# Weight sums of a Winograd down projection made ahead during the up projection and kept in HBM, with another order of its products

## The chip, the cores and the metric

The kernel runs on one core of one Trainium2 chip. The metric is the device time of one execution in microseconds (us), as the median of several runs. A profile is one further execution, recorded by the hardware profiler, with its own time.

## The reference

The reference is a two-layer encoder trunk on x of 1024 tokens by 1024 channels in float32. Each layer is a mixer and then a gated feed-forward part; the change touches only the latter:

```
def conv_ffn(h, w_up, conv_w, conv_b, w_down):        # D_FF = 2816
    z = causal_dwconv(h @ w_up, conv_w, conv_b)       # width 3 along the tokens
    a, g = jnp.split(z, 2, axis=-1)
    return (jax.nn.silu(g) * a) @ w_down
x = x + conv_ffn(rms_norm(x, ffn_norm_g[l]), ...)     # l = 0, 1
```

## The kernel before

**Products.** Activations are held transposed: channels on the 128 partitions, tokens along the free dimension, in two halves of 512 tokens (h = 0, 1). Every float32 operand is split in a high part (a cast to fp32r, on ACT) and a low part (source minus high part, on DVE or POOL), and a product is three matmuls: high by high, high by low, low by high (`matmul3`, L328). So each operand costs ACT a cast and DVE or POOL a subtraction.

**Seven products in place of eight.** The two large matrix products of the feed-forward part are done as 2x2 block products in Winograd's form, with seven products, numbered p = 1 to 7, of sums of blocks of both operands. In the up projection (`up`, L508) one `Quad` makes one channel tile j of the value and of the gate (22 quads a layer, NF = 22); a quad is seven products of 12 matmuls. POOL makes the weight sums (L363 to L369) and all low parts of weights (L353), ACT the high parts (L352). DVE evicts: `qe_u` (L402) and `c_u` (L409, the program's c22) add partial sums, then the width-3 convolution is one ACT instruction (L542) and two DVE instructions (L544) for each part and half, three single-column ACT instructions at the border of the halves (L561), and the gate is an ACT sigmoid (L565) and two DVE products for each half (L566, L567). The gated tile z goes to HBM (`hid_d`, L569). Product p=4 of a quad accumulates in the bank `qb` that `c_u` reads, so it waits for `c_u`.

**The down projection** (`down`, L583) reads the gated tiles back. Its contraction runs over NP = 11 pairs of channel tiles, i; one step (p, i) is four output tiles q of three matmuls, 12 matmuls. Order: products 1 and 5 interleaved (5 lags by two steps), then 6 and 3 the same way, then 7, 2, 4. The operands:

- `hidden(i)` (L588) loads both tiles of a pair with both halves at once, 2 x 512 KB, in the first two products; 22 tiles then stay in SBUF. `operand` (L644) makes the sums of blocks on DVE, in place (`hid<-hid`), and the split (`set`, L318 and L319).
- `operand_w` (L611) loads blocks of the weight, 256 KB each (`d<-in_w_down`). For p = 5, 6 and 3 it also makes sums of blocks: one POOL addition for 5; a POOL and a DVE subtraction for 6, and a store of one sum to HBM (L633) that p = 7 loads again; one POOL subtraction for 3. Each product's weights get a cast (L640) and a low part on POOL.

Tiles come from rings: 4 raw weight tiles and 8 split ones (two pools each, taken in turn), 3 tiles `z`, 28 activation tiles. In PSUM the accumulator A uses the tags qa and qb, B uses qe and pp, two banks each.

**What sets the order.** Tile's scheduler orders each engine's instructions at build time, mostly in the order of the program, with earlier places for work that it finds ready; an engine then runs its list strictly in order. Loads and stores sit in one list, SP's (a few of the program's first loads in ACT's). `later(n, fn)` puts work into the program after n further steps (a step is three matmuls in the feed-forward part), `sooner(n)` raises a priority.

Of the kernel before, what the change touches and what calls it, by code (L numbers as in the profile page):

```python
# [17 lines left out]
P = 128  # L18
# [23 lines left out]
NORM_LAG = ((8, 10), (6, 5))  # L42
EPS = 1e-6
# [24 lines left out]
def trunk_kernel(ctx: ExitStack, tc: tile.TileContext, a: dict, out: bass.AP):  # L68
# [11 lines left out]
    now = {"turn": {}}  # L80

    @contextmanager
    def stage(name, psum):

        with (
            tc.tile_pool(name=name, bufs=1, reuse_waits="tile") as mp,
            tc.tile_pool(name=f"ps_{name}", bufs=psum, space=PSUM, reuse_waits="tile") as pp,
        ):
            now.update(mp=mp, pp=pp)
            yield mp  # L90
# [16 lines left out]
    def ps(name):  # L107
        return now["pp"].tile([P, HS], F32, tag="pp", name=name)
# [336 lines left out]
    def run_quads(quads, n_early):  # L445
        for i, q in enumerate(quads[:n_early]):
            q.ready(i == 0)
        for q in quads[:n_early]:
            q.early()
        for q in quads[:n_early]:  # L450
            q.late()
        n = len(quads)
        order = [(n_early, 1), (n_early, 5)]
        for i in range(n_early, n):
            order += [(i, 6), (i, 2), (i + 1, 1), (i, 7), (i, 3), (i + 1, 5), (i, 4)]
        for i, p in order:
            if i < n:
                quads[i].step(p)
# [49 lines left out]
    def up(layer, sets, hid_d):  # L508
# [15 lines left out]
        def evict(j):  # L524
# [10 lines left out]
            def fn(part, h, src):  # L535
# [26 lines left out]
                if len(done) == 4:  # L562
                    for h in range(2):
                        sg = ps(f"sg{layer}_{j}{h}")
                        nc.scalar.activation(sg, z[1][h], AF.Sigmoid)  # L565
                        nc.vector.tensor_tensor(sg, z[1][h], sg, op=ALU.mult)  # L566
                        nc.vector.tensor_tensor(z[0][h], z[0][h], sg, op=ALU.mult)  # L567
                    if j < NF - 2:
                        nc.sync.dma_start(hid_d[j], z[0][2])  # L569
                    else:  # L570
                        stores.append(lambda: nc.sync.dma_start(hid_d[j], z[0][2]))
# [3 lines left out]
        run_quads([Quad(f"u{layer}_{j}", load(j), sets, evict(j)) for j in range(NF)], EARLY)  # L575
        return stores

# [5 lines left out]
    def down(layer, hid_d, nxt, fin, stores):  # L583
        A, B = [[None] * 4 for _ in range(2)]
        hid, two_raw, s2 = {}, {}, {}
        s3_d = [tc.dram_tile([P, HS], F32, name=f"s3_{layer}_{i}") for i in range(NP)]

        def hidden(i):  # L588

            if i not in hid:  # L590
                b = []
                for f in (2 * i, 2 * i + 1):
                    t = actp.tile([P, 2, HS], F32, tag="act", name=f"hid{layer}_{f}")
                    nc.sync.dma_start(t, hid_d[f])
                    b += [t[:, 1], t[:, 0]]
                hid[i] = b
            return hid[i]

        def raw(tag, srcs, name):
            t = ffn_buf(tag, F32, f"d{name}_{layer}")  # L600
            for k, src in enumerate(srcs):
                made = nc.sync.dma_start(t[:, k], src)
            return t, made

        def block(r, c, i):
            return a["w_down"][layer, r, c, i]

        def tt(eng, o, one, two, op=ALU.subtract):
            eng.tensor_tensor(o, one, two, op=op)  # L609

        def operand_w(p, i):  # L611

            if p in (1, 2, 4, 7):

                if i % 2 == 0:
                    ii = range(i, min(i + 2, NP))
                    srcs = [s3_d[k] if p == 7 else block(*{1: (0, 0), 2: (0, 1), 4: (1, 1)}[p], k) for k in ii]
                    two_raw[p], made = raw("raw", srcs, f"{p}_{i}")
                    if stores and i == 2:
                        with tc.issue_after(made.ins):  # L620
                            while stores:
                                stores.pop(0)()
                src = two_raw[p][:, i % 2]
            elif p == 5:
                t, _ = raw("raw", [block(1, 0, i), block(1, 1, i)], f"5_{i}")
                src = t[:, 0]
                tt(nc.gpsimd, src, src, t[:, 1], ALU.add)
            elif p == 6:
                t, _ = raw("raw", [block(0, 0, i), block(1, 0, i)], f"6_{i}")
                z, _ = raw("z", [block(1, 1, i), block(0, 1, i)], f"3_{i}")  # L630
                s3, src = t[:, 0], t[:, 1]
# [3 lines left out]
                s2[i] = z[:, 1], src  # L635
            else:
                src, s2_i = s2.pop(i)
                tt(nc.gpsimd, src, src, s2_i)
            t = ffn_buf("hl", F32R, f"w{p}_{layer}_{i}")
            nc.scalar.copy(t[:, 0], src)  # L640
            tt(nc.gpsimd, t[:, 1], src, t[:, 0].bitcast(F32))
            return t[:, 0], t[:, 1]

        def operand(p, i):  # L644
            b11, b12, b21, b22 = hidden(i)
            if p == 5:
                tt(nc.vector, b11, b12, b11)
            elif p == 6:
                tt(nc.vector, b11, b22, b11)
            elif p == 7:  # L650
                tt(nc.vector, b12, b22, b12)
            src = {1: b11, 5: b11, 6: b11, 3: b22, 7: b12, 2: b21, 4: b21}[p]
            s = {p: []}
            put_set(s, p, src, nc.vector)
            if p == 2:
                tt(nc.vector, b21, b21, b11)
# [7 lines left out]
        def step(p, i):  # L664
            O, first = {1: (A, True), 6: (A, False), 7: (A, False), 5: (B, True), 3: (B, False), 2: (B, True)}[p]
            first = first and i == 0
            W, X = operand_w(p, i), operand(p, i)
            for q in range(4):
                if first:
                    tag = (("qa", "qa", "qb", "qb"), ("qe", "qe", "pp", "pp"))[O is B][q]  # L670
# [17 lines left out]
        def two(p, r, after_p, after_r):  # L688
            for i in range(NP + 2):
# [4 lines left out]
                if i >= 2:  # L694
                    step(r, i - 2)
            after_r()

        def x12():
            takes(A, 0, 0)
# [3 lines left out]
        for i in range(NP):  # L703
            step(7, i)
        takes(A, 1, 0, True)
        for i in range(NP):
            step(2, i)
        takes(B, 0, 1, True)
# [4 lines left out]
        for i in range(NP):  # L713
            ops.append((operand_w(4, i), operand(4, i)))
            if i < tail:
                for q in range(4):
                    product(q, A, *ops[i], False, False)
# [6 lines left out]
    def ffn(layer, sets, nxt, fin):  # L724
        hid_d = [tc.dram_tile([P, 2, HS], F32, name=f"hid{layer}_{j}") for j in range(NF)]
        with (
# [4 lines left out]
            stores = up(layer, sets, hid_d)  # L731
            down(layer, hid_d, nxt, fin, stores)
# [431 lines left out]
```

## Time and profile before

| | |
|---|---|
| median of 3 runs | 1938.11 us (1936.58 to 1938.32) |
| profiled execution | 1944.7 us, of which the span from first to last instruction 1943.0 us |
| granted TensorE clock, mean | 0.979 of full speed |
| busy: PE, DVE, ACT, POOL | 95%, 61%, 48%, 67% of the span |
| DMA | 200.22 MB, mean 103 GB/s |

The two feed-forward parts run from about 289 to 966 us and from about 1259 to 1926 us. In layer 0 the first matmul of the down projection starts at 726.9 us and the last at 965.8 us; in layer 1 at 1689.6 and 1925.5 us. PE's busy time is modelled, because matmuls overlap in its pipeline: a matmul of 512 columns shows as 0.39 us long, and at full clock one starts every 0.2267 us. So lost time is found by counting matmuls in a stretch, not by the busy share.

### The profile page before, as it was taken

The numbers are of one execution on the slowest core, as the hardware profiler recorded it, in microseconds if no ns is written. First come the engines' busy times: TensorE is split into PE (matmuls) and PEld (weight loads), VectorE is DVE, ScalarE is ACT, GpSimd is POOL, SyncE is SP. The second block draws the span as 40 slices with busy tenths as digits, with TensorE's granted clock in tenths as the row PEclk, the third lists the DMA queues.
The fourth block names the chain that finished last, engine by engine and source line by source line (L and its number), as shares of the span: only waits on it lengthen the run. The fifth ranks groups of instructions, "written<-read, shape, count | busy, mean of one in ns | idle before, by whom it ended". The sixth has DMA issues, their size and how long they took to land. (4 is left out here: it accounts for less than half of the span.)

```text
span 1943.0 us, 22672 instructions
## 1 busy us (share of the span) xinstructions
PE 1849.3 (95%) x8088; PEld 1508.5 (78%) x8092; DVE 1190.0 (61%) x1540; ACT 930.7 (48%) x1684; POOL 1302.4 (67%) x946
## 2 busy tenths in 40 slices
PE   8999889999999997999999999999999999798997
PEld 6777667888888876778778888878888888686786
DVE  5899788455554586768620256584555554957784
ACT  6436445555555563345321233365555555532451
POOL 2899567877777775885432446587777777658851
PEclk8999989999999998999999999999999999999998
DMA  4111130222222267543111323202122222865432
GB/s 152 44 54 33 44 98 23 88 96 76 88 82 81 90 233 241 188 145 111 49 54 48 95 86 119 87 30 90 67 96 76 87 85 78 291 216 181 131 98 87
DMA packets 79395, 200.22 MB, mean 103 GB/s; under 512 B 8497, under 2 KB 9521, under 8 KB 79281
## 3 DMA queue, kind: packets, MB, share of 16 engines
q1 hardware_dynamic: 78992, 198.48, 30.5%
q8 instruction: 64, 1.05, 0.2%
q14 instruction: 51, 0.41, 0.1%
q10 hardware_dynamic: 288, 0.28, 0.0%
HBM read 165.70 MB, written 33.03 MB: 102 GB/s over the span
## 5 line engine op out<-in xcount | busy, mean ns | idle before, releaser
L353 POOL TENSOR_TENSOR w_u<-S_u,w_u 128x512 fp32r<-128x512 f32 x160 | 207.4, 1296 | 113.2 <-ACT w_u L352 110.7
L609 POOL TENSOR_TENSOR w<-d,w 128x512 fp32r<-128x512 f32 x154 | 234.3, 1537 | 72.9 <-ACT w L640 72.6
L329 PE MATMUL p<-set,w 128*128 128x512 f32 x616 | 244.2, 396 | 29.7 <-ACT z L561 19.3
L331 PE MATMUL p<-set,w 128*128 128x512 f32 x616 | 243.3, 395 | 6.1 <-POOL w L609 6.1
L330 PE MATMUL p<-set,w 128*128 128x512 f32 x616 | 243.8, 396 | 1.8 <-DVE set L319 1.6
L319 DVE TENSOR_TENSOR set<-hid,set 128x512 fp32r<-128x512 f32 x154 | 162.7, 1077 | 58.3 <-ACT set L318 57.8
L353 POOL TENSOR_TENSOR w_u<-r_u,w_u 128x512 fp32r<-128x512 f32 x120 | 156.1, 1302 | 58.1 <-ACT edge L555 42.4
L329 PE MATMUL qb_u<-set,w_u 128*128 128x512 f32 x480 | 188.4, 393 | 6.4 <-DVE c_u L409 6.3
L331 PE MATMUL qb_u<-set,w_u 128*128 128x512 f32 x480 | 188.2, 392 | 0.0
L330 PE MATMUL qb_u<-set,w_u 128*128 128x512 f32 x480 | 188.0, 392 | 0.0
L640 ACT CAST w<-d 128x512 fp32r<-128x512 f32 x154 | 94.4, 618 | 178.5 <-DVE d L609 105.4
L329 PEld LDWEIGHTS p<-set,w 128*128 128x128 f32 x616 | 117.4, 191 | 59.0 <-ACT z L561 20.2
L544 DVE SCALAR_TENSOR_TENSOR z<-qb_u,cols,z 128x511 f32<-128x511 f32 x88 | 65.8, 748 | 142.0 <-ACT z L542 140.6
L331 PEld LDWEIGHTS p<-set,w 128*128 128x128 f32 x616 | 117.4, 191 | 33.5 <-POOL w L609 9.3
L352 ACT CAST w_u<-S_u 128x512 fp32r<-128x512 f32 x160 | 98.5, 616 | 93.1 <-PE qb_u L331 60.1
L330 PEld LDWEIGHTS p<-set,w 128*128 128x128 f32 x616 | 117.3, 190 | 29.1 <-DVE set L319 5.2
L331 PE MATMUL qa_u<-set,w_u 128*128 128x512 f32 x320 | 124.6, 389 | 0.6 <-POOL w_u L353 0.6
L329 PE MATMUL qa_u<-set,w_u 128*128 128x512 f32 x320 | 124.6, 389 | 0.0
L330 PE MATMUL qa_u<-set,w_u 128*128 128x512 f32 x320 | 124.5, 389 | 0.0
L329 PE MATMUL qe_u<-set,w_u 128*128 128x512 f32 x320 | 124.5, 389 | 0.0
L330 PE MATMUL qe_u<-set,w_u 128*128 128x512 f32 x320 | 124.5, 389 | 0.0
L331 PE MATMUL qe_u<-set,w_u 128*128 128x512 f32 x320 | 124.5, 389 | 0.0
(241 smaller groups left out, 4729.1 us busy)
## 6 DMA issues: line engine op xcount, KB each, us to landing
d<-in_w_down SPq DMA_DIRECT2D x198, 256.0 KB, 3.0
r_u<-in_w_up SPq DMA_DIRECT2D x88, 512.0 KB, 3.3
hid<-z SPq DMA_DIRECT2D x44, 512.0 KB, 2.6
hid<-hid SPq DMA_DIRECT2D x44, 512.0 KB, 5.5
r_wv<-in_od_in SPq DMA_DIRECT2D x16, 512.0 KB, 3.8
r_odo<-in_od_out SPq DMA_DIRECT2D x16, 512.0 KB, 3.3
s<-d SPq DMA_DIRECT2D x22, 256.0 KB, 3.0
d<-s SPq DMA_DIRECT2D x22, 256.0 KB, 3.8
```

Of the source, the lines that this page charges most:

```text
L319: leng.tensor_tensor(t[:, 1], src, t[:, 0].bitcast(F32), op=ALU.subtract)
L329: nc.tensor.matmul(o, H, xH, start=first, stop=False, skip_group_check=True)
L330: nc.tensor.matmul(o, H, xL, start=False, stop=False, skip_group_check=True)
L331: nc.tensor.matmul(o, L, xH, start=False, stop=last, skip_group_check=True)
L352: nc.scalar.copy(H, src)
L353: nc.gpsimd.tensor_tensor(L, src, H.bitcast(F32), op=ALU.subtract)
L544: nc.vector.scalar_tensor_tensor(o[:, s:], src[:, : HS - s], w[2 - s], o[:, s:], op0=ALU.mult, op1=ALU.add)
L609: eng.tensor_tensor(o, one, two, op=op)
L640: nc.scalar.copy(t[:, 0], src)
```

## The change

1. A new function, `weight_sums`, is started in the up projection after the first two quads. It goes through the down weights in 22 chunks (pair i, half of the columns). A chunk is two loads of 256 KB in pieces of 1 KB (`ws<-in_w_down`), four DVE instructions of 128x256 with both operands in SBUF, and two stores of 256 KB to HBM (`sums_d`). The buffers are two tiles for each of the tags acc and sq.
2. `operand_w` makes no sums any more. It loads either a block or a finished sum, two pairs i by one DMA of 512 KB, and makes the split; every third tile from the seventh on comes from the ring `z`. The additions on POOL and DVE in p = 5, 6 and 3 and the eleven stores and loads of `s3` are gone.
3. The order of the products is 2 with 1 (lagging by three steps), 5 with 6, 3 with 7 (each lagging by two), then 4.
4. Gated tiles lie in HBM as (pair, tile, half) and are loaded by halves: 512 KB of the half h = 1 in the products 2 and 1, the half h = 0 in 5 and 6.
5. The splits of p = 1, and of p = 2 from the fourth step on, are queued behind the last gate instructions on ACT and DVE (`issue_after`).
6. A uses the PSUM tags qb and pp, B uses qe and qa; the statistics of the next norm use qe during p = 4, and four of their squares move into p = 4.

```diff
+SUM_STEPS = 22
-    def run_quads(quads, n_early):
+    def run_quads(quads, n_early, then):
...
         for q in quads[:n_early]:
             q.late()
+        later(SUM_STEPS, then)
...
+                    now["gate"] = on_act.ins, on_dve.ins
+                    def store():
+                        nc.sync.dma_start(hid_d[j // 2][:, j % 2], z[0][2])
...
+    CHUNKS = 2 * NP
+    def weight_sums(layer, sums_d):
+        w = a["w_down"][layer]
+        def loads(n):
+            i, cs = n // 2, slice(n % 2 * 2 * P, (n % 2 + 1) * 2 * P)
+            ts = []
+            for c, tag in enumerate(("acc", "sq")):
+                t = npool.tile([P, 2, 2 * P], F32, tag=tag, name=f"ws{c}_{layer}_{n}", bufs=2)
+                nc.sync.dma_start(t, w[:, c, i, :, cs].rearrange("r p c -> p r c"))
+                ts.append(t)
+            def sums():
+                (a11, a21), (a12, a22) = [[t[:, r] for r in range(2)] for t in ts]
+                tt(nc.vector, a22, a21, a22, ALU.add)
+                tt(nc.vector, a21, a11, a21)
+                tt(nc.vector, a11, a22, a11)
+                tt(nc.vector, a12, a12, a11)
+                for t, d in zip(ts, sums_d):
+                    nc.sync.dma_start(d[i // 2][:, :, i % 2, cs], t)
+            return sums
+        def go(n, sums=None):
+            if sums:
+                sums()
+            if n < CHUNKS:
+                made = loads(n)
+                later(SUM_STEPS, lambda: go(n + 1, made))
+        go(0)
...
+        def hidden(i, h):
+            d = one if h else two_
+            if i not in d:
+                t = actp.tile([P, 2, HS], F32, tag="act", name=f"hid{h}_{layer}_{i}")
+                nc.sync.dma_start(t, hid_d[i][:, :, h])
+                d[i] = [t[:, 0], t[:, 1]]
+            return d[i]
         def operand_w(p, i):
...
-                tt(nc.gpsimd, src, src, t[:, 1], ALU.add)
...
-                tt(nc.gpsimd, s3, s3, src)
-                nc.sync.dma_start(s3_d[i], s3)
-                tt(nc.vector, src, z[:, 0], s3)
...
-                tt(nc.gpsimd, src, src, s2_i)
+            if i % 2 == 0:
+                n = min(2, NP - i)
+                own = n_raw[0] % 3 == 0 if n_raw[0] >= 6 else None
+                t = ffn_buf("z" if own else "raw", F32, f"d{p}_{layer}_{i}")
+                n_raw[0] += 1
+                if p in (1, 2, 4):
+                    r, c = {1: (0, 0), 2: (0, 1), 4: (1, 1)}[p]
+                    src = a["w_down"][layer, r, c, i : i + n].rearrange("i p c -> p i c")
+                else:
+                    k, r = {6: (0, 0), 7: (0, 1), 3: (1, 0), 5: (1, 1)}[p]
+                    src = sums_d[k][i // 2][:, r, :n]
+                made = nc.sync.dma_start(t[:, :n], src)
...
+            with ExitStack() as order:
+                if p == 1 or (p == 2 and i >= 3):
+                    for ins in now["gate"]:
+                        order.enter_context(tc.issue_after(ins))
+                W, X = operand_w(p, i), operand(p, i)
...
-        two(1, 5, lambda: takes(A, 0, 1), lambda: takes(B, 1, 0))
-        two(6, 3, x12, lambda: takes(B, 0, 0, True))
...
+        two(2, 1, 3, lambda: takes(B, 0, 1), lambda: takes(A, 0, 1))
+        two(5, 6, 2, lambda: takes(B, 1, 0), lambda: takes(A, 0, 0))
+        two(3, 7, 2, lambda: takes(B, 0, 0, True), lambda: takes(A, 1, 0, True))
+
+        now["spare"] = "qe"
```

**How it moves instructions.** Three places of the engines' lists follow. Line numbers are those of the file that the list belongs to.

DVE in the up projection of layer 0, from quad 3's `c_u` on. L409 and L413 are `c_u`, L544 and L549 the convolution; `ws` are the chunks' tiles, with the chunk's number third from the end. Before:

```order
L409 TENSOR_TENSOR c_u_3_2994<-qb_u_3_2821,s_u_3_2886 128x512
L544 SCALAR_TENSOR_TENSOR z_0_3_2996<-c_u_3_2994,cols,z_0_3_2996 128x511
L544 SCALAR_TENSOR_TENSOR z_0_3_2996<-c_u_3_2994,cols,z_0_3_2996 128x510
L544 SCALAR_TENSOR_TENSOR z_0_3_2949<-qe_u_3_2873,cols,z_0_3_2949 128x511
L544 SCALAR_TENSOR_TENSOR z_0_3_2949<-qe_u_3_2873,cols,z_0_3_2949 128x510
L544 SCALAR_TENSOR_TENSOR z_0_3_2996<-qb_u_3_2821,cols,z_0_3_2996 128x511
L544 SCALAR_TENSOR_TENSOR z_0_3_2996<-qb_u_3_2821,cols,z_0_3_2996 128x510
L402 TENSOR_TENSOR qe_u_4_3027<-qb_u_4_2975,s_u_4_3040 128x512
```

Now:

```order
L413 TENSOR_TENSOR c_u_3_3009<-qb_u_3_2822,s_u_3_2891 128x512
L627 TENSOR_TENSOR ws_0_7_3746<-ws_0_7_3746,ws_0_7_3744 128x256
L549 SCALAR_TENSOR_TENSOR z_0_3_3011<-c_u_3_3009,cols,z_0_3_3011 128x511
L549 SCALAR_TENSOR_TENSOR z_0_3_3011<-c_u_3_3009,cols,z_0_3_3011 128x510
L549 SCALAR_TENSOR_TENSOR z_0_3_2964<-qe_u_3_2878,cols,z_0_3_2964 128x511
L549 SCALAR_TENSOR_TENSOR z_0_3_2964<-qe_u_3_2878,cols,z_0_3_2964 128x510
L627 TENSOR_TENSOR ws_0_8_3887<-ws_0_8_3885,ws_0_8_3887 128x256
L627 TENSOR_TENSOR ws_0_8_3885<-ws_0_8_3885 128x256
L627 TENSOR_TENSOR ws_0_8_3885<-ws_0_8_3887,ws_0_8_3885 128x256
L627 TENSOR_TENSOR ws_0_9_4011<-ws_0_9_4009,ws_0_9_4011 128x256
L627 TENSOR_TENSOR ws_0_8_3887<-ws_0_8_3887,ws_0_8_3885 128x256
L627 TENSOR_TENSOR ws_0_9_4009<-ws_0_9_4009 128x256
```

The sums stand between the evictions, four chunks (16 instructions) in each of the quads 2 to 6; the last of the 22 chunks stands in quad 6, although the program spaces them over nearly the whole up projection.

SP in the same part of layer 0. `r_u` are up weights, `hid<-z` the store of a gated tile. Before:

```order
L518 DMA r_u_1_5_3111<-in_w_up 128x1024
L569 DMA hid_2_2283<-z_0_2_2795 128x1024
L518 DMA r_u_0_6_3263<-in_w_up 128x1024
L518 DMA r_u_1_6_3265<-in_w_up 128x1024
L569 DMA hid_3_2284<-z_0_3_2949 128x1024
```

Now:

```order
L603 DMA ws_0_6_3620<-in_w_down 128x2x256
L613 DMA sums_0_1_2293<-ws_0_5_3488 256x1x256
L523 DMA r_u_1_5_3136<-in_w_up 128x1024
L613 DMA sums_1_1_2299<-ws_0_5_3490 256x1x256
L603 DMA ws_0_6_3622<-in_w_down 128x2x256
L603 DMA ws_0_7_3744<-in_w_down 128x2x256
L603 DMA ws_0_7_3746<-in_w_down 128x2x256
L575 DMA hid_1_2282<-z_0_2_2796 128x1024
L523 DMA r_u_0_6_3298<-in_w_up 128x1024
L613 DMA sums_0_1_2293<-ws_0_6_3620 256x1x256
```

Up weights and gated tiles now queue behind stores that wait for DVE and behind loads that wait for the landing of such a store.

DVE at the end of the up projection of layer 0, from the last quad's `c_u` on (`set<-hid` and `hid<-hid` are the down projection's). Before:

```order
L409 TENSOR_TENSOR c_u_21_5743<-qb_u_21_5593,s_u_21_5658 128x512
L544 SCALAR_TENSOR_TENSOR z_0_21_5720<-qa_u_21_5580,cols,z_0_21_5720 128x510
L609 TENSOR_TENSOR hid_6_5918<-hid_6_5918 128x512
L319 TENSOR_TENSOR set<-hid_8_5966,set 128x512
L319 TENSOR_TENSOR set<-hid_4_5869,set 128x512
L609 TENSOR_TENSOR hid_2_5842<-hid_3_5844,hid_2_5842 128x512
L544 SCALAR_TENSOR_TENSOR z_0_21_5720<-qe_u_21_5645,cols,z_0_21_5720 128x511
L609 TENSOR_TENSOR hid_6_5918<-hid_7_5920,hid_6_5918 128x512
L544 SCALAR_TENSOR_TENSOR z_0_21_5745<-c_u_21_5743,cols,z_0_21_5745 128x511
L609 TENSOR_TENSOR hid_8_5966<-hid_8_5966 128x512
L609 TENSOR_TENSOR hid_4_5869<-hid_5_5871,hid_4_5869 128x512
L544 SCALAR_TENSOR_TENSOR z_0_21_5745<-qb_u_21_5593,cols,z_0_21_5745 128x511
```

Now:

```order
L413 TENSOR_TENSOR c_u_21_5964<-qb_u_21_5814,s_u_21_5879 128x512
L549 SCALAR_TENSOR_TENSOR z_0_21_5966<-c_u_21_5964,cols,z_0_21_5966 128x511
L549 SCALAR_TENSOR_TENSOR z_0_21_5966<-c_u_21_5964,cols,z_0_21_5966 128x510
L549 SCALAR_TENSOR_TENSOR z_0_21_5941<-qe_u_21_5866,cols,z_0_21_5941 128x511
L549 SCALAR_TENSOR_TENSOR z_0_21_5941<-qe_u_21_5866,cols,z_0_21_5941 128x510
L549 SCALAR_TENSOR_TENSOR z_0_21_5966<-qb_u_21_5814,cols,z_0_21_5966 128x511
L549 SCALAR_TENSOR_TENSOR z_0_21_5966<-qb_u_21_5814,cols,z_0_21_5966 128x510
L571 TENSOR_TENSOR sg_210_6012<-z_0_21_5966,sg_210_6012 128x512
L572 TENSOR_TENSOR z_0_21_5941<-z_0_21_5941,sg_210_6012 128x512
L571 TENSOR_TENSOR sg_211_6016<-z_0_21_5966,sg_211_6016 128x512
L572 TENSOR_TENSOR z_0_21_5941<-z_0_21_5941,sg_211_6016 128x512
L323 TENSOR_TENSOR set<-hid_0_3_6093,set 128x512
```

Before, nineteen instructions of the down projection stand between `c_u` and the last gate product (the list goes on for 19 rows to it); now none does. Only three `set`s, for the first three steps of p = 2, stand further up, among the evictions of quad 20.

## Rows read from the trace of the kernel before

**Rows 1.** Windows by stretch: a steady quad, then six stretches around the down projections.

```profile
core 0: us, PE busy (x) PEld busy (x) DVE busy (x) ACT busy (x) POOL busy (x), PEclk, DMA share, GB/s
441.50:460.54 19.04, 19.04 (x85) 15.77 (x84) 9.97 (x14) 11.07 (x22) 14.09 (x12) 1.00 0.25 83
718.00:747.00 29.00, 15.42 (x52) 11.77 (x51) 29.00 (x39) 12.01 (x25) 11.39 (x8) 0.76 0.76 273
797.00:817.00 20.00, 16.51 (x64) 12.17 (x63) 14.92 (x17) 3.74 (x7) 17.43 (x13) 0.91 0.59 197
842.00:862.00 20.00, 16.91 (x70) 12.33 (x69) 10.90 (x11) 9.57 (x19) 15.21 (x11) 1.00 0.46 148
1682.00:1704.00 22.00, 9.97 (x30) 7.53 (x30) 22.00 (x29) 10.67 (x22) 9.51 (x7) 0.74 0.81 305
1760.00:1782.00 22.00, 15.72 (x65) 11.47 (x64) 16.92 (x18) 4.81 (x9) 19.71 (x14) 1.00 0.60 197
1794.00:1826.00 32.00, 28.79 (x120) 21.69 (x119) 16.54 (x18) 15.61 (x29) 25.31 (x17) 1.00 0.50 152
```

**Rows 2.** Waits of PE from 690 to 985 us.

```profile
PE p L329 <- ACT z L561: 10.4, 1, 10.4
PE qb_u L329 <- DVE c_u L409: 3.2, 1, 3.2
PE p L331 <- POOL w L609: 3.0, 3, 1.3
PE p L329 <- ACT w L640: 2.1, 1, 2.1
```

**Rows 3.** Timeline at the end of layer 0's up projection, PE and ACT.

```profile
739.49 0.79 PE L329 MATMUL p<-set,w 128*128 128x512 f32 x1 [10.36 <-ACT z L561]
...
738.08 0.35 ACT L561 ACTIVATE z<-qb_u,z,cols 128x1 f32<-128x1 f32 x1 [5.30 <-DVE z L544]
```

**Rows 4.** Instructions on the tiles d: ns min/median/max, first and last start.

```profile
L609 POOL TENSOR_TENSOR d<-d x44: 1266/1362/1808, 703.6 to 1802.4; 128x512 f32<-128x512 f32 x44
...
L609 POOL TENSOR_TENSOR d<-d,d x22: 1281/1620/1681, 782.8 to 1818.6; 128x512 f32<-128x512 f32 x22
```

**Rows 5.** DVE by form, and the window, from 870 to 925 us.

```profile
L319 DVE TENSOR_TENSOR set<-hid,set 128x512 fp32r<-128x512 f32 x22 | 21.6, 997 | 4.1 <-ACT set L318 3.9
L609 DVE TENSOR_TENSOR hid<-hid,hid 128x512 f32<-128x512 f32 x11 | 12.3, 1123 | 0.1
...
L679 DVE TENSOR_TENSOR x<-p,x 128x512 f32<-128x512 f32 x8 | 5.1, 677 | 0.0
...
870.00:925.00 55.00, 55.00 (x245) 45.53 (x243) 44.22 (x48) 27.73 (x50) 33.77 (x23) 1.00 0.36 110
```

**Rows 6.** DVE by form from 745 to 800 us.

```profile
L609 DVE TENSOR_TENSOR hid<-hid,hid 128x512 f32<-128x512 f32 x11 | 15.6, 1429 | 0.3
```

**Rows 7.** DVE by form in the steady quad, 441.5 to 460.6 us.

```profile
L544 DVE SCALAR_TENSOR_TENSOR z<-qb_u,cols,z 128x511 f32<-128x511 f32 x1 | 0.7, 749 | 3.9 <-ACT z L542 3.9
...
L409 DVE TENSOR_TENSOR c_u<-qb_u,s_u 128x512 f32<-128x512 f32 x1 | 0.7, 700 | 3.1 <-PE qb_u L331 3.1
```

**Rows 8.** Timeline of the same quad: `c_u`, and p=4's first matmul.

```profile
452.58 0.70 DVE L409 TENSOR_TENSOR c_u<-qb_u,s_u 128x512 f32<-128x512 f32 x1 [3.09 <-PE qb_u L331]
...
457.82 0.39 PE L329 MATMUL qb_u<-set,w_u 128*128 128x512 f32 x1
```

**Rows 9.** DVE by form in the first 60 us: the one 128x256 form.

```profile
L166 DVE TENSOR_TENSOR L_first<-r_first,H_first 128x256 fp32r<-128x256 f32 x4 | 1.7, 422 | 3.2 <-ACT H_first L165 3.1
```

**Rows 10.** DMA issues from 727 to 800 us: count, KB each, median us to landing.

```profile
d<-in_w_down SPq DMA_DIRECT2D x35, 256.0 KB, 3.4
...
s<-d SPq DMA_DIRECT2D x4, 256.0 KB, 2.0
```

**Rows 11.** Timeline of PE after a wait: first and last of seven slow matmuls.

```profile
723.05 0.63 PE L331 MATMUL qb_u<-set,w_u 128*128 128x512 f32 x1
...
725.61 0.63 PE L331 MATMUL qb_u<-set,w_u 128*128 128x512 f32 x1
```

More of the change, by code (lines that the diff above doesn't have):

```diff
@@ L78, in trunk_kernel @@
     weights = {t: ctx.enter_context(tc.tile_pool(name=t, bufs=n)) for t, n in BUFS.items()}
-    now = {"turn": {}}
+    now = {"turn": {}, "spare": None}
     @contextmanager
@@ L88, in stage @@
         ):
-            now.update(mp=mp, pp=pp)
+            now.update(mp=mp, pp=pp, spare=None)
             yield mp
@@ L107, in ps @@
     def ps(name):
+        if now["spare"]:
+            return bank(now["spare"], name)
         return now["pp"].tile([P, HS], F32, tag="pp", name=name)
@@ L506, in trunk_kernel, with up @@
     EARLY = 2
-    def up(layer, sets, hid_d):
+    def up(layer, sets, hid_d, sums_d):
         stores = []
@@ L568, in fn @@
+                    def store():
+                        nc.sync.dma_start(hid_d[j // 2][:, j % 2], z[0][2])
                     if j < NF - 2:
-                        nc.sync.dma_start(hid_d[j], z[0][2])
+                        store()
                     else:
-                        stores.append(lambda: nc.sync.dma_start(hid_d[j], z[0][2]))
+                        stores.append(store)
             return fn
-        run_quads([Quad(f"u{layer}_{j}", load(j), sets, evict(j)) for j in range(NF)], EARLY)
@@ new lines, in up @@
+        run_quads(
+            [Quad(f"u{layer}_{j}", load(j), sets, evict(j)) for j in range(NF)],
+            EARLY,
+            lambda: weight_sums(layer, sums_d),
+        )
+        return stores
+    CHUNKS = 2 * NP
[24 more added lines that the diff above has]
+        go(0)
@@ new lines, in tt, with down @@
+    def tt(eng, o, one, two, op=ALU.subtract):
+        eng.tensor_tensor(o, one, two, op=op)
+    def down(layer, hid_d, sums_d, nxt, fin, stores):
+        A, B = [[None] * 4 for _ in range(2)]
+        one, two_, raws = {}, {}, {}
+        n_raw = [0]
+        def hidden(i, h):
[5 more added lines that the diff above has]
+            return d[i]
+        def operand_w(p, i):
+            if i % 2 == 0:
[10 more added lines that the diff above has]
+                made = nc.sync.dma_start(t[:, :n], src)
+                if stores and i == 2:
+                    with tc.issue_after(made.ins):
+                        while stores:
+                            stores.pop(0)()
+                raws[p] = t
+            src = raws[p][:, i % 2]
@@ L644, in operand @@
         def operand(p, i):
-            b11, b12, b21, b22 = hidden(i)
+            b11, b21 = hidden(i, 1)
+            b12, b22 = hidden(i, 0) if p not in (1, 2) else (None, None)
             if p == 5:
@@ L685, in takes, with two @@
                 take(O, q, part, h, final)
-        def two(p, r, after_p, after_r):
-            for i in range(NP + 2):
+        def two(p, r, lag, after_p, after_r):
+            for i in range(NP + lag):
                 if i < NP:
@@ L714, in down @@
             ops.append((operand_w(4, i), operand(4, i)))
+            if i == 3:
+                for q in range(4):
+                    nxt.feed(2 * q, 1)
             if i < tail:
@@ L724, in ffn @@
     def ffn(layer, sets, nxt, fin):
-        hid_d = [tc.dram_tile([P, 2, HS], F32, name=f"hid{layer}_{j}") for j in range(NF)]
+        hid_d = [tc.dram_tile([P, 2, 2, HS], F32, name=f"hid{layer}_{i}") for i in range(NP)]
+        sums_d = [
+            [tc.dram_tile([P, 2, 2, HS], F32, name=f"sums{layer}_{k}_{i}") for i in range((NP + 1) // 2)]
+            for k in range(2)
+        ]
         with (
@@ L730, in ffn @@
             now.update(pq=pq, primed={})
-            stores = up(layer, sets, hid_d)
-            down(layer, hid_d, nxt, fin, stores)
+            stores = up(layer, sets, hid_d, sums_d)
+            down(layer, hid_d, sums_d, nxt, fin, stores)
             while pend and layer == NB - 1:
```

66 lines of the change are left out of this document (8 added, 58 removed).

## The prediction

> **What bounds the kernel now.** I read the windows first, then PE's waits, then the timelines of whoever is waited for. In a steady quad of the up projection PE starts 84 matmuls in 19.04 us, 0.2267 us each (the row counts one more at its border), with no idle time: there PE is the bound [rows 1]. Around the down projections it is not. A stretch has lost its length less 0.2267 us for every matmul started in it. For layer 0 that gives 29.0 - 52 x 0.2267 = 17.2 us at the start of the down projection, 5.5 at its first change of products and 4.1 in products 6 and 3, together 26.8; for layer 1 15.2, 7.3 and 4.8, together 27.3 [rows 1]. So at most 54.1 us, 2.8% of the run, lie open to any change of this stage.
>
> The reader should see two causes. At the start PE waits 3.2 us for `c_u` and 10.4 us for ACT's border columns [rows 2], and ACT in turn stood 5.3 us behind DVE [rows 3]: DVE is busy for all 29.0 of 29.0 us [rows 1], because the last evictions share its list with sums and splits of the down projection. Later PE waits for POOL's low parts and for weight casts [rows 2], in stretches where POOL is busy 17.4 of 20 us and 19.7 of 22 [rows 1].
>
> Both have a common root. A DVE instruction with one operand in PSUM takes 677 ns; one with both in SBUF takes 997 or 1123 ns on average while POOL is busy 33.8 of 55 us [rows 5], and 1429 in a busier stretch [rows 6]. So each two-SBUF instruction waits for POOL, by about (21.6 + 12.3) / 33 - 0.68 = 0.35 us [rows 5], and POOL for it.
>
> **What goes.** Per layer the down projection loses 33 additions on POOL (44 and 22 in the two layers, 1.36 and 1.62 us [rows 4]: some 48 us), 11 subtractions on DVE, and 11 stores with their loads. Each of its steps then needs one POOL instruction, near 1.5 us, against 2.72 us of matmuls (12 x 0.2267). In the first stage DVE holds two `set`s a pair of steps, 2 x 1.03 us against 5.44, where it held a `set` more and the sums of blocks, and half the gated bytes are loaded there. In 5 with 6 the new list holds six two-SBUF instructions a pair (the sums for 7 and 4 are moved up): 6.2 us against 5.44, late by 0.75 x 11 = 8 us. I cost that at nothing, since DVE enters with a lead: the eight split weight tiles allow eight steps, 21.8 us. Without that lead it would cost the 8 us.
>
> At the start DVE has ten instructions from `c_u` to the gate's end and nothing between. The three steps of p = 2 that are prepared earlier give PE 3 x 2.72 = 8.2 us of cover. From the last up product to the gate's end I count an ACT eviction, two convolutions, border columns and two gates, some 6 us by the durations of one quad; then a cast and a split, 1.6. That just fits. I leave 1 us for it, and 1 us for each of two changes of products where an accumulator must be read before it is written on: 3 us a layer, bounds 0 and 8. The four squares that move into p = 4, the other PSUM tags and the stores of the last gated tiles change no count, and I take 0; p = 4 holds one `set` a step as before, and four additions that found no room there would cost 4 x 1.1 us at most.
>
> **What comes.** 22 chunks a layer. By the list of DVE they stand not over the whole up projection but in quads 2 to 6, 16 instructions a quad. A 128x256 subtraction takes 422 ns where nothing disturbs it [rows 9]. In the up projection DVE now has no two-SBUF instruction, so the wait for POOL is new there. Ends: 0 (every sum falls where POOL stands idle) and 0.75 us (1429 less 677 ns [rows 6]). I take 0.35 [rows 5], since the load of POOL is then nearest: 16 x (0.42 + 0.35) = 12.3 us on top of 9.97 makes a quad of 22.3 us, of which POOL's 14.09 [rows 1] are 63%, and in rows 5 POOL had 61%.
>
> DVE is free for 19.04 - 9.97 = 9.1 us of a quad [rows 1], in two gaps mostly, 3.9 us ahead of `qb`'s eviction and 3.1 ahead of `c_u` [rows 7]. So it falls behind by 12.3 - 9.1 = 3.2 us a quad. Behind a late DVE stand ACT's border columns, the next `qe_u` and `c_u`; the first to be missed is `c_u`, which ends at 453.28 where p = 4 starts at 457.82 [rows 8]: 4.5 us of slack. From quad 2's `c_u` to quad 6's there are four quads: 4 x 3.2 - 4.5 = 8.3 us of waits of PE, some 3 us in each of three quads. After quad 6 the list is clean and DVE catches up.
>
> A wait of that length costs more than itself: behind the 3.2 us wait at 722.5 us the granted clock falls to the lower level, 1.2 GHz (0.76 of 2.4 on average in that stretch [rows 1]), and seven matmuls start 0.43 us apart in place of 0.227 [rows 11]; with the ones at the edges 1.6 us. Three times: 4.8. So the up projection pays 13.1 us a layer.
>
> The chunks' DMAs are 88 a layer on SP. Two buffers of each tag make a ring: last sum, store, load, first sum of the chunk after next. Landings of 256 KB took 2.0 us for a store and 3.4 for a load at a busier time [rows 10], 5.4 together, against about 9.5 us (half a quad) less three for the sums. I take 0; each us more in the landing would cost 2 us a quad, 8 a layer. A gated tile's store now waits behind such loads; its tile is needed again only in the next quad's `c_u` eviction, and I take 0 for that too.
>
> **Sum.** 54.1 - 2 x 3 - 2 x 13.1 = 21.9 us less, on the profiled execution's 1944.7 us: 1922.8. The median of the runs is 6.6 us lower, so the forecast is 1938.1 - 21.9, about 1916 us.
>
> For the wait of DVE on POOL there is a stated rule. The Trainium skill, page SBUF — State Buffer, section on the two separate sides, says that a DVE instruction with two SBUF inputs and a GpSimd instruction that reads SBUF take one port pair as an exclusive lock for a whole instruction, and the loser fully blocks. The trace agrees in kind: 677 against 997 to 1429 ns. Read as "each sum waits on average for half of a POOL instruction of 1.28 us, whenever POOL is busy", it would give 0.64 x 0.63 = 0.40 us, and a forecast of about 1923 us; read at its worst it is rival C.
>
> **Rivals.**
> A, the forecast: the up projection pays 4 to 22 us a layer; 1900 to 1934. 45%.
> B, the sums fit: the scheduler put them into the gaps, POOL stands idle 5 us a quad [rows 1], and if the wait is below 0.15 us, 16 x 0.57 = 9.1 us fit the free 9.1. Then 54.1 - 6 = 48 us less: 1890. For it: the gap ahead of `c_u` coincides with idle POOL. Against it: rows 5. 22%.
> C, slower: DVE alternates with POOL. The gap of 3.9 us lies where POOL works back to back, and there a sum can wait a whole POOL instruction. With the mean wait of rows 6, 0.75 us, it is 16 x 1.17 = 18.7 us, 9.6 behind a quad, 4 x 9.6 - 4.5 + 4.8 = 38.7 a layer, and 54.1 - 6 - 77 = 29 us more: 1967. The change turns from gain to loss at 24 us a layer, that is at a wait of 0.52 us. For it: rows 6; against it: a quad that PE lengthens dilutes POOL. 18%.
> D, the change does not do what it says at the start: DVE is clear, but p = 1 and the fourth step of 2 wait for the gate's end and then for cast, split and loads, and half of the 54.1 us stays. 54.1 / 2 - 26 = 1 us less: 1937. 12%. The other 3% are none of these.
>
> **Numbers.** A measurement of this kernel can tell about 0.2%, 3.9 us, from no change: the borders are 1934.2 and 1942.0. Faster: 0.41 of A, all of B, 0.03 of D: 0.66. Same: 0.08 of D, 0.02 each of A and C, 0.02 of the rest: 0.14. Slower: 0.20. The range that should hold 8 of 10 leaves out most of C above and a little of B below: 1888 to 1946; A's own is 1900 to 1934.
>
> **What would show it.** Right: no wait of PE for ACT's border columns at the start of the down projections, POOL at one instruction a step there, waits of PE for `c_u` of about 3 us in three quads near 365 to 450 us and again some 970 us later, `ws` instructions of 0.7 to 0.8 us, and a dip of the granted clock there. B shows PE without waits in those quads; C shows `ws` instructions above 1 us. A `ws` instruction that waits for its load would put the price on the ring of buffers and not on POOL. The forecast is wrong if the six quads run clean, or if PE still loses over 8 us a layer in the down projection.

## The result, and the profile after

The changed kernel takes 1981.82 us (median of 4 runs, 1980.05 to 1985.15) against 1938.21 us for the kernel before on the same chip: ratio 1.0227, 95% interval [1.021, 1.0245]. It is slower by 43.6 us. The forecast was 1916 us, range 1888 to 1946: wrong in sign and outside its range. The profiled execution took 1980.05 us, span 1978.1 us.

The first view is the windows: a quad in which chunks stand, then the start of the down projection and its changes of products in layer 0 (757 to 842 us), then the same two for layer 1. They answer to [rows 1].

```profile
core 0: us, PE busy (x) PEld busy (x) DVE busy (x) ACT busy (x) POOL busy (x), PEclk, DMA share, GB/s
408.58:436.59 28.01, 22.34 (x84) 17.61 (x84) 21.70 (x30) 10.70 (x23) 14.80 (x11) 0.87 0.62 207
757.00:786.00 29.00, 29.00 (x130) 24.02 (x129) 21.03 (x24) 18.09 (x36) 15.03 (x10) 1.00 0.61 219
820.00:842.00 22.00, 18.58 (x74) 14.52 (x73) 21.97 (x30) 6.77 (x13) 12.50 (x8) 0.92 0.43 132
1736.00:1758.00 22.00, 22.00 (x99) 18.22 (x98) 16.47 (x20) 12.49 (x26) 8.44 (x6) 1.00 0.47 162
1796.00:1820.00 24.00, 19.33 (x83) 15.03 (x83) 24.00 (x31) 8.10 (x15) 13.01 (x8) 1.00 0.39 121
```

The down projections now start without a loss: 130 matmuls in 29.0 us and 99 in 22.0 are what 0.2267 us a matmul gives, where [rows 1] had 52 in 29.0 and 30 in 22.0. The changes of products lose 22.0 - 74 x 0.2267 = 5.2 us and 24.0 - 83 x 0.2267 = 5.2. The rest of them loses nothing that the counts show (546 matmuls in the 123 us from 842 us on, 487 in the 110 us from 1820 us on). So 54.1 us of losses became 10.4: 43.7 gained. All of that and as much again is lost in the up projection: a quad that took 19.04 us takes 28.01.

PE's waits over the whole run name both deadlines of that quad:

```profile
PE qb_u L333 <- DVE qe_u L406: 38.4, 12, 5.4
PE qb_u L333 <- DVE c_u L413: 19.4, 8, 4.6
...
PE qa_u L335 <- POOL w_u L357: 0.6, 1, 0.6
```

The last line speaks against a third cause: the up weights, whose loads now queue behind the chunks' stores, reach PE late only once, by 0.6 us. The waits for ACT's border columns and for POOL's low parts of [rows 2] are gone from the down projections. DVE's groups of the form of the sums, from 350 to 500 us (count, busy us, mean ns, then the idle time ahead of them and what ended it), and the DMAs of the chunks there:

```profile
L627 DVE TENSOR_TENSOR ws<-ws,ws 128x256 f32<-128x256 f32 x63 | 45.5, 742 | 30.0 <-DMA ws<-in_w_down 27.4 <-issue 2.1
L627 DVE TENSOR_TENSOR ws<-ws 128x256 f32<-128x256 f32 x21 | 20.5, 975 | 0.3
```

```profile
sums<-ws SPq DMA_DIRECT2D x42, 256.0 KB, 2.5
ws<-in_w_down SPq DMA_DIRECT2D x40, 256.0 KB, 4.0
```

A sum takes (45.5 + 20.5) / 84 = 0.79 us, 0.77 was forecast. But DVE also stands 30.0 us ahead of them for loads, which was costed at nothing. DVE's timeline in one such quad shows both, ahead of a late `qe_u`; below it stand PE's first matmul behind that `qe_u`, and then POOL's timeline:

```profile
395.41 0.75 DVE L549 SCALAR_TENSOR_TENSOR z<-qe_u,cols,z 128x510 f32<-128x510 f32 x1
398.31 0.42 DVE L627 TENSOR_TENSOR ws<-ws,ws 128x256 f32<-128x256 f32 x1 [2.15 <-DMA ws<-in_w_down]
398.77 1.40 DVE L627 TENSOR_TENSOR ws<-ws 128x256 f32<-128x256 f32 x1
400.21 4.25 DVE L627 TENSOR_TENSOR ws<-ws,ws 128x256 f32<-128x256 f32 x3
404.38 1.48 DVE L627 TENSOR_TENSOR ws<-ws 128x256 f32<-128x256 f32 x1
...
407.89 0.69 DVE L406 TENSOR_TENSOR qe_u<-qb_u,s_u 128x512 f32<-128x512 f32 x1
...
413.58 0.49 DVE L627 TENSOR_TENSOR ws<-ws,ws 128x256 f32<-128x256 f32 x1 [3.29 <-DMA ws<-in_w_down]
```

```profile
408.72 0.77 PE L333 MATMUL qb_u<-set,w_u 128*128 128x512 f32 x1 [5.18 <-DVE qe_u L406]
```

```profile
397.14 1.29 POOL L368 TENSOR_TENSOR S_u<-S_u,r_u 128x512 f32<-128x512 f32 x1
398.40 1.49 POOL L357 TENSOR_TENSOR w_u<-S_u,w_u 128x512 fp32r<-128x512 f32 x1
399.86 1.47 POOL L357 TENSOR_TENSOR w_u<-r_u,w_u 128x512 fp32r<-128x512 f32 x1
401.29 1.47 POOL L372 TENSOR_TENSOR S_u<-r_u,r_u 128x512 f32<-128x512 f32 x1
402.72 1.46 POOL L357 TENSOR_TENSOR w_u<-S_u,w_u 128x512 fp32r<-128x512 f32 x1
```

From 398.8 to 405.9 us DVE and POOL go by turns, one DVE sum of 1.40 us per POOL instruction of 1.47. So two causes lie side by side: the two-buffer ring (DVE waits for loads) and the turns with POOL. The mean of 0.79 us hides sums of 0.42 and of 1.40.

### The profile page after: what moved, and what is told of

Read it like the earlier page. It is cut to its first block, busy times and chain, and to the rows that moved or that the text cites. A ratio compares the mean times of both kernels' runs of the same rounds, so it can differ in the third digit from the quotient of the medians.

```text
span 1978.1 us, 22750 instructions
## 1 busy us (share of the span) xinstructions
PE 1859.4 (94%) x8088; PEld 1516.3 (77%) x8092; DVE 1280.2 (65%) x1694; ACT 925.0 (47%) x1684; POOL 1209.6 (61%) x880
## 5 line engine op out<-in xcount | busy, mean ns | idle before, releaser
L627 POOL TENSOR_TENSOR w<-d,w 128x512 fp32r<-128x512 f32 x154 | 228.7, 1505 | 194.4 <-ACT w L669 190.5
L357 POOL TENSOR_TENSOR w_u<-S_u,w_u 128x512 fp32r<-128x512 f32 x160 | 211.5, 1322 | 175.9 <-ACT w_u L356 169.7
L333 PE MATMUL qb_u<-set,w_u 128*128 128x512 f32 x480 | 197.4, 411 | 57.9 <-DVE qe_u L406 38.4
L335 PE MATMUL qb_u<-set,w_u 128*128 128x512 f32 x480 | 194.5, 405 | 0.0
L334 PE MATMUL qb_u<-set,w_u 128*128 128x512 f32 x480 | 194.1, 404 | 0.0
L322 ACT CAST set<-hid 128x512 fp32r<-128x512 f32 x154 | 91.2, 618 | 172.1 <-DVE hid L627 104.4
L333 PEld LDWEIGHTS qb_u<-set,w_u 128*128 128x128 f32 x480 | 94.7, 197 | 86.5 <-ACT z L566 33.6
L627 DVE TENSOR_TENSOR ws<-ws,ws 128x256 f32<-128x256 f32 x132 | 97.2, 755 | 57.3 <-DMA ws<-in_w_down 53.8
L549 DVE SCALAR_TENSOR_TENSOR z<-qb_u,cols,z 128x511 f32<-128x511 f32 x88 | 65.8, 747 | 104.1 <-ACT z L547 102.7
L335 PE MATMUL qa_u<-set,w_u 128*128 128x512 f32 x320 | 124.6, 389 | 0.6 <-POOL w_u L357 0.6
L333 PE MATMUL qe_u<-set,w_u 128*128 128x512 f32 x320 | 124.9, 390 | 0.0
L333 PE MATMUL qa_u<-set,w_u 128*128 128x512 f32 x320 | 124.6, 389 | 0.0
L334 PE MATMUL qe_u<-set,w_u 128*128 128x512 f32 x320 | 124.6, 389 | 0.0
```

The lines of the kernel that those rows point to most:

```text
L333: nc.tensor.matmul(o, H, xH, start=first, stop=False, skip_group_check=True)
L334: nc.tensor.matmul(o, H, xL, start=False, stop=False, skip_group_check=True)
L335: nc.tensor.matmul(o, L, xH, start=False, stop=last, skip_group_check=True)
L357: nc.gpsimd.tensor_tensor(L, src, H.bitcast(F32), op=ALU.subtract)
L549: nc.vector.scalar_tensor_tensor(o[:, s:], src[:, : HS - s], w[2 - s], o[:, s:], op0=ALU.mult, op1=ALU.add)
```

## The experiments

Each edit is against the changed kernel. "Quad" below is the time from one `qe_u` to the next, or the window of it. A result called single is one timed execution. On one of the chips the kernel before took 1932.4 to 1947.5 us in seven runs, so a difference of a few us between single runs says little.

**What is the new down projection worth alone?** The chunks are left out.

```diff
-            lambda: weight_sums(layer, sums_d),
+            lambda: None,
...
-                    src = sums_d[k][i // 2][:, r, :n]
+                    src = a["w_down"][layer, r, k, i : i + n].rearrange("i p c -> p i c")
```

> The changed kernel without the chunks: no loads, sums or stores in the up projection; the down projection loads plain blocks of the weight where it would load finished sums (products 6, 7, 3 and 5 so use other weights, in the same number of bytes). What is left of the change is its new down projection. By the two traces the down projections and the ends of the up projections lose some 23 us a layer less than before, and the quads in which the chunks stand lose 45.8 and 38.4 us more. Every theory that blames the chunks expects 1938 - 46 = 1892 us, 1885 to 1900; were part of the loss in the new order of products, 1910 or more.

Measured: 1894.46 us, ratio to before 0.9771 [0.9755, 0.9787], 44.9 us less than the kernel before on the same chip (1939.32). The new down projection is worth what the windows said, and the chunks cost 1981.82 - 1894.46 = 87.4 us.

**Ring alone.** The sums become instructions with one SBUF operand, at the same places of DVE's list:

```diff
-                tt(nc.vector, a22, a21, a22, ALU.add)
...
+                for o, s in ((a22, a21), (a21, a11), (a11, a22), (a12, a11)):
+                    nc.vector.tensor_reduce(
+                        o, s.rearrange("p (c k) -> p c k", k=1), axis=mybir.AxisListType.X, op=ALU.add
+                    )
```

> The same list of DVE as in the changed kernel, the same loads, stores and ring, but each of the four sums of a chunk is an instruction with a single SBUF operand (a reduction over an axis of length one, 128x256; the sums are not formed). Theory 1, alternation with POOL: the instructions take about 0.4 us everywhere, PE's waits for qe_u (38.4 us in the changed kernel) mostly go and with them the slow clock behind them, 1905 to 1940 us. Theory 2, the ring: the waits for loads stay and so do PE's waits, 1970 to 1985 us.

Measured: 1942.9 us (a single timed run), between the two expectations. DVE's group, 350 to 500 us, and PE's waits over the run:

```profile
L609 DVE TENSOR_REDUCE ws<-ws 128x256 f32<-128x256 f32 x84 | 32.9, 415 | 41.4 <-DMA ws<-in_w_down 37.3 <-issue 3.3
```

```profile
PE qb_u L333 <- DVE c_u L413: 15.7, 9, 3.0
...
PE qb_u L333 <- DVE qe_u L406: 10.0, 8, 2.1
```

The window of one quad:

```profile
404.38:426.92 22.54, 18.69 (x81) 15.23 (x82) 15.19 (x31) 10.70 (x22) 12.20 (x11) 1.00 0.77 257
```

With one operand an instruction takes 415 ns beside a busy POOL. DVE is busy only 15.2 us of a quad, and still the quad takes 22.5 us, because DVE stands for loads. The ring alone costs 1942.9 - 1894.5 = 48 us.

**Sums alone, two places.** Two resident pairs of tiles, no ring. In the first run the sums are queued behind `c_u` and behind the gate:

```diff
-SUM_STEPS = 22
+SUM_STEPS = 7
...
+            ts = now["kept"][n % 2] if n > 1 else []
...
+                with tc.issue_after(now["pin"]):
                     tt(nc.vector, a22, a21, a22, ALU.add)
...
-                for t, d in zip(ts, sums_d):
-                    nc.sync.dma_start(d[i // 2][:, :, i % 2, cs], t)
```

(`now["pin"]` is the `c_u` or the last gate product, whichever was issued last.)

> The sums without a ring: only the first two chunks of a layer are loaded, nothing is stored, and all 22 chunks do their four sums on those resident tiles, two chunks behind c_u and two behind the last gate product of each of quads 2 to 6; the down projection loads plain blocks as in the run without chunks. Theory 1, alternation with POOL: eight sums ahead of qe_u at up to 1.40 us are 11.2 us against 3.9 us of gap and 4.5 us of slack, so some 2.8 us of wait and 1.6 of slow clock in each of five quads a layer, 44 us above the run without chunks, 1915 to 1945 us, with PE waiting for qe_u. Theory 2, the ring: no load to wait for, at most 5 us above the run without chunks, below 1900 us.

Measured: 1911.5 us (a single run), 17 above the run without chunks and between the two expectations. In one quad of the trace (402.6 to 422.8 us) the eight sums behind `c_u` take 3.9 us, 0.49 each: four of them run while POOL stands idle. The eight behind the gate take 6.1 us, 0.77 each, and the quad 20.25 us. This is not the place of the changed kernel, whose list has eight of a quad's sixteen sums behind the convolution of `qe_u`. The second run has them where the changed kernel has them:

```diff
+        tiles = [loads(n) for n in range(2)]
+        def do(ins):
+            for n in range(2):
+                if n_done[0] < CHUNKS:
+                    n_done[0] += 1
+                    with tc.issue_after(ins):
+                        tiles[n]()
...
+                if (part, h) == (0, 1) and j > EARLY:
+                    now["do"](on_dve.ins)
```

(and the same call behind the last gate product.)

> The sums without a ring once more, now at the very place where the changed kernel has them: two chunks (eight sums) behind the second convolution of qe_u, where POOL works back to back, and two behind the last gate product, in quads 3 to 8 of each layer, on two resident pairs of tiles; no further loads, no stores, plain blocks in the down projection. In the run before this one the sums stood behind c_u and cost 17 us over the run without chunks (1911.5 against 1894.5). Additive theory: the ring alone cost 48 us (1942.9), so the rest of 87 us, some 39, is the alternation with POOL at this place: 1925 to 1940 us. Theory that the 4.5 us of slack swallow the alternation and only both together overrun it: eight sums at up to 1.40 us are 11.2, less the gap of 3.9 and the slack, 2.8 us at most in a quad: 1900 to 1918 us.

Measured: 1952.5 us (a single run), 58 above the run without chunks and beyond both expectations. DVE's timeline ahead of one `qe_u`, and the window of the quad that begins with it:

```profile
404.45 2.72 DVE L631 TENSOR_TENSOR ws<-ws,ws 128x256 f32<-128x256 f32 x2
407.09 2.94 DVE L631 TENSOR_TENSOR ws<-ws 128x256 f32<-128x256 f32 x2
409.96 2.52 DVE L631 TENSOR_TENSOR ws<-ws,ws 128x256 f32<-128x256 f32 x4
412.40 1.52 DVE L549 SCALAR_TENSOR_TENSOR z<-qb_u,cols,z 128x511 f32<-128x511 f32 x2
413.84 0.69 DVE L406 TENSOR_TENSOR qe_u<-qb_u,s_u 128x512 f32<-128x512 f32 x1
```

```profile
413.84:438.42 24.58, 20.96 (x84) 16.67 (x84) 22.94 (x31) 10.69 (x22) 15.04 (x11) 0.93 0.17 64
```

DVE is busy 22.94 of 24.58 us, the rest are waits for ACT. Without any load to wait for, DVE's list bounds the quad: 24.58 - 19.04 = 5.5 us over PE's time, in five and a half quads a layer (22 chunks, four a quad): 61 us in both layers, less a part of the slack, against 58 measured.

**Ring and sums together, at that place.** Stores and loads put back:

```diff
+                    tiles[n][1]()
+                    if n_done[0] + 2 < CHUNKS:
+                        tiles[n] = loads(n_done[0] + 2)
```

(`tiles[n][1]()` stores the pair.)

> The run with the sums at the changed kernel's place on resident tiles (1952.5 us), with the ring put back: each pair of chunks is stored after its sums and the next pair loaded into the same two buffers; nothing is left out. If the ring pays on top of DVE's own overload: in each of ten gaps between two bursts of eight sums a layer DVE stands some 3 us for a load, as in the changed kernel (53.8 us in all), and 20 to 40 us come on top: 1972 to 1992 us. If DVE's own overload is the whole of it and the changed kernel's waits for loads only fill time that DVE lost anyway: 1950 to 1960 us.

Measured: 1974.3 us (a single run), inside the first expectation and 21.8 us above the run on resident tiles. But 5.1 of these us arise before any chunk: the first product of the steady quads starts at 343.8 us in place of 338.7. From that product to the last instruction the runs take 1551.8 us without chunks, 1598.0 with the ring alone, 1611.9 with the sums alone, 1628.8 with both, and 1638.9 in the changed kernel. So the ring pays on top, with 17 us, below the 20 to 40 that were expected, and both together at this place stay 10 us short of the changed kernel. A quad:

```profile
420.85:446.62 25.77, 20.88 (x84) 16.61 (x84) 21.97 (x31) 10.69 (x22) 14.84 (x11) 0.93 0.68 224
```

DVE's larger group of sums from 350 to 500 us:

```profile
L639 DVE TENSOR_TENSOR ws<-ws,ws 128x256 f32<-128x256 f32 x54 | 44.0, 838 | 11.7 <-DMA ws<-in_w_down 10.6 <-issue 0.6
```

DVE stands 11.7 us ahead of these sums, nearly all for loads, where it stood 30.0 in the changed kernel. The list here has eight sums on either side of `c_u`; there it has seven and nine. Whether that makes the 10 us was not tested.

**Fewer chunks a quad.** One line of difference: each chunk's sums are queued behind the last gate product, so the scheduler cannot bring them forward.

```diff
+                with tc.issue_after(now["gate"][1]):
                     tt(nc.vector, a22, a21, a22, ALU.add)
```

> Each chunk's four sums are queued behind the last gate product of the quad before, so that DVE has one or two chunks in each of the quads 3 to 19, in the gap ahead of c_u where POOL stands idle, in place of four a quad in quads 2 to 6, half of them ahead of qe_u where POOL works back to back. Theory 1, DVE and POOL alternate (sums of 1.40 us in place of 0.42): every sum takes about 0.42 us, PE waits neither for qe_u nor for c_u, 1890 to 1900 us. Theory 2, the ring of two buffers (DVE waits 53.8 us for loads): with one chunk in 16 to 19 us the round trip has time enough, also 1890 to 1900 us. Theory 3, the 23 MB more of DMA traffic hold up the weights of the up projection: the loss is spread but stays, 1930 us or more.

Measured: 1900.61 us, ratio to before 0.9801 [0.9786, 0.9816], 0.6 us above what theories 1 and 2 expected. From 340 us to the down projection of layer 0 the trace shows no wait of PE at all. DVE's groups from 350 to 500 us:

```profile
L628 DVE TENSOR_TENSOR ws<-ws,ws 128x256 f32<-128x256 f32 x27 | 18.9, 724 | 0.2
L628 DVE TENSOR_TENSOR ws<-ws 128x256 f32<-128x256 f32 x9 | 7.3, 824 | 0.0
```

No wait for a load is left, but the sums take (18.9 + 7.3) / 36 = 0.73 us, so theory 1's "about 0.42 us" is wrong: they still meet POOL, and it costs nothing, because DVE has time. Theory 3 falls: the same 223 MB are moved. This version beats both kernels. Next the same number of chunks, queued behind `c_u` (`now["c22"]` is that instruction), which was meant to put them into POOL's busy stretch:

```diff
+                with tc.issue_after(now["c22"]):
```

> The full work again (loads, sums, stores) spread over quads 2 to 19, one or two chunks a quad, but queued behind c_u, so that they stand in the stretch ahead of qe_u where POOL works back to back. Theory 1 at full price: in each of four quads a layer with two chunks eight sums at 1.40 us overrun gap and slack by 2.8 us, with the slow clock 4.4, 35 us in all: 1930 to 1940 us. Theory of gap and slack: one chunk (5.6 us) fits, two nearly, so within 6 us of the run with the sums behind the gate (1900.6): 1898 to 1907 us, with PE waiting for qe_u for under 1 us in all.

Measured: 1900.92 us, 0.9801 [0.977, 0.9832], and no wait for `qe_u`. At one or two chunks a quad it makes no difference which of the two instructions the sums are queued behind. As a test of POOL's busy stretch the run is weak: in a quad with two chunks the sums run from 415.5 to 422.2 us and POOL works back to back only from 419.0 us on, and the mean of a sum from 350 to 500 us is 0.73 us, as in the run before. Then two and three chunks a quad, behind the gate (`SUM_STEPS = 14`, `SUM_STEPS = 9`):

> As the run with the sums behind the gate, but two chunks in each quad, quads 3 to 13, in place of one or two in 3 to 19. If the ring costs whenever DVE comes back to a pair of tiles before store and load (2.5 and 4.0 us in the changed kernel) have landed, nothing changes, since DVE comes back after some 16 us: 1898 to 1907 us. If its cost goes with the density of chunks and transfers, half of the 48 us of the ring-only run show: 1915 to 1930 us.

> The full work with the sums behind the gate products as in the run of 1900.6 us, but three chunks in a quad, quads 2 to 8, in place of one or two. By DVE's time: twelve sums at 0.6 to 0.86 us are 7.2 to 10.3 us against 9.1 us free in a quad, so the edge: with the ring's round trip hidden, 1898 to 1915 us, PE waiting for c_u or qe_u by 1 us in a quad at most. If the ring already bites at three chunks (a third pair of tiles is wanted within one burst), 1920 to 1950 us, with DVE waiting for loads.

Measured: 1909.4 and 1960.6 us, a single run each, the first between its two expectations and the second above both of its own. A quad of the first; then a quad of the second, and the first sum of a third chunk there:

```profile
413.15:432.19 19.04, 19.04 (x85) 15.77 (x84) 13.95 (x23) 11.27 (x24) 14.44 (x12) 1.00 0.57 193
```

```profile
423.38:446.92 23.54, 19.59 (x84) 15.61 (x84) 20.06 (x28) 10.70 (x22) 15.00 (x11) 1.00 0.62 201
```

```profile
440.12 1.15 DVE L628 TENSOR_TENSOR ws<-ws,ws 128x256 f32<-128x256 f32 x1 [1.44 <-DMA ws<-in_w_down]
```

With two chunks PE runs clean; its 9 us over the run of 1900.6 arise ahead of the steady quads (their first product starts at 347.6 us in place of 338.8; the mixer before, in which no chunk stands, is late by 5.4 us at 195.7 us and by 8.1 at 237.1; from that product to the end it is 1560.0 against 1559.2 us). With three, which the expectation took for the edge, DVE is busy 20.06 us, over PE's 19.04, and stands for loads and for ACT on top: the third chunk lands in the busy stretch and its load is not there. Each sum adds (13.95 - 9.97) / 8 = 0.50 us to DVE's busy time with two chunks and (20.06 - 9.97) / 12 = 0.84 with three. The dear ones are the third chunk's: its four sums, ahead of `qe_u`, take 5.4 us (1.34 each), the eight ahead of `c_u` also 5.4 (0.67 each).

## Why the prediction was wrong, step by step

**The down projection: right.** It gave 48 us (54.1 less 3 a layer); the run without chunks shows 44.9. The 3 us a layer were 5.2: nothing at the start, all of it at the changes of products, where PE waits for DVE to read an accumulator (`x<-p,x`, 3.4 us in layer 0 and 4.7 in layer 1). No border columns are waited for, so rival D falls.

**The price of a sum: right in size, in part by luck.** 0.77 us forecast, 0.79 measured, as a mean of sums of 0.42 and of 1.40 us; the same sums take 0.86 us on average at that place without the ring. DVE is busy 21.70 us in a quad where 9.97 + 12.3 = 22.3 were forecast.

**The step that failed: "I take 0" for the ring of chunk buffers.** A quad was to take 22.3 us, DVE's busy time; it takes 28.01. The 30.0 us in [350, 500] are 30.0 / (150 / 28.01) = 5.6 us a quad, which is that difference. The step knew the price, 2 us a quad for each us that a landing is too long, and took the excess as nothing. Its landing was short: the trace has 2.5 + 4.0 = 6.5 us, not 5.4. That alone would have cost nothing by its own account, since the time for it was taken as 6.5 us, half a quad less one chunk's sums, as if the chunks stood evenly. They stand in bursts that use both pairs of buffers back to back, and the loads wait in SP's list. SP's timeline from 390 to 440 us has in the quad shown above:

```profile
401.64 5.22 SPq L613 DMA_DIRECT2D sums<-ws  x3
406.91 0.60 SPq L603 DMA_DIRECT2D ws<-in_w_down  x1
407.61 0.52 SPq L613 DMA_DIRECT2D sums<-ws  x1
408.18 0.60 SPq L603 DMA_DIRECT2D ws<-in_w_down  x1
```

The first chunk of the burst has its last sum at 404.46 us (400.21 + 4.25), and after the gate, at 410.30, DVE wants the buffer again: 5.8 us later. The chunk's second store, the second of the three in the first line, is issued at 404.49 and has landed at 406.92. The load into that buffer stands in SP's list behind the store of the burst's last sum, which ends at 407.31, so it is issued at 408.18; it lands at 413.56, and DVE begins at 413.58. The round trip took 9.1 us, and DVE stood 3.29. At the burst before that, SP's order cost next to nothing: sum to 391.33, store landed at 394.24, load issued at 394.25 and landed at 398.29. That is 7.0 us, where DVE was back after 4.8 (396.16), and it stood 2.15. So two waits of 2 to 3 us arise in a quad. How much of them a third pair of buffers, or loads in a list without such stores, would take away was not tested. DVE's list, which has 7 sums between `qe_u` and `c_u` and 9 between `c_u` and the next `qe_u`, was read for its count alone.

**A second step was too small by itself.** All of DVE's idle time, 9.1 us, was taken as free, and the lateness as 4 x 3.2 - 4.5 us a layer. With no ring, sums at the changed kernel's place cost 58 us, where the forecast had 2 x 13.1 (2 x 8.3 without the slow matmuls): a sum cost 0.86 us there, DVE still had to wait for ACT (24.58 - 22.94 = 1.6 us a quad), and five and a half quads paid in place of four. So without the ring the forecast would still have been too low, at 1952 us against 1916. That is 29 us a layer, between A's 4 to 22 and C's 38.7. The turns with POOL are those of rival C, but not its price: C took 1.17 us a sum in four quads. The two causes overlap: 58 and 48 alone make 106, together they make 87.4 in the changed kernel and 79.8 in the run with both put back.

**The clock was no term of its own.** The forecast added 4.8 us a layer for slow matmuls behind waits. In the quad of 28.01 us the granted clock is 0.87 of 2.4 GHz on average, so PE ran at the lower level, 1.2 GHz, for a part of it, but 21.70 us busy and 6.3 idle on DVE fill the quad: none of DVE's waits in that quad is for PE, so a faster PE would have waited for the next `qe_u` or `c_u` all the same. No run isolates the clock. With ring alone the quad takes 22.54 us at a granted clock of 1.00.

**The deadline** was named as `c_u`; PE waits for `qe_u` twice as long (38.4 against 19.4 us), since the turns with POOL stand ahead of `qe_u` (with the ring alone, `c_u` comes first: 15.7 against 10.0). This changes the place, not the sum.

**Rival B's** 1890 us is what the same sums cost when they are spread: 1900.6. Its remaining 6 us over the run without chunks lie in the down projections (226.0 against 220.6 us from the first product to the next stage in layer 0); there PE waits 3.6 us for DVE's splits (`set`) against 1.5. Why these come later was not followed further.

## What to carry to other kernels

Work that is put "into the gaps" of an engine with a strict order needs three numbers in one quad: the engine's busy time with the new work, the waits in it that nothing can fill, and for every buffer the time from its last use to its next first use against a full round trip, with what stands ahead of its load in the list of DMAs. Read the scheduled list for bursts, not for counts: a program that spaces its chunks over the whole stage is no promise, and one line that held them back turned 1.0227 into 0.9801. Cost at nothing only what has shown slack in that very place.

## What the runs showed of the hardware

DVE and POOL by turns do not share the loss evenly. While they alternate, a POOL instruction goes from 1.29 to 1.47 us and a DVE sum from 0.42 to 1.40: the shorter instruction pays nearly all. A single-operand reduction of the same size took 415 ns on average with POOL busy 99.8 of 150 us, as a subtraction that nothing disturbs (422 ns [rows 9]), so no wait shows. The Trainium skill, page SBUF — State Buffer, section on the two separate sides, states the exclusive lock for two SBUF inputs and says that the other engine "fully blocks"; the 1.40 and 1.47 us by turns agree in kind. What that comes to in a mean depends on the place: in a quad of the run without a ring the eight sums ahead of `qe_u`, where POOL works back to back, take 8.2 us (1.02 each) and the eight ahead of `c_u` 5.6 us (0.70 each).
